# Four of eight experts with 64 token slots, chosen on the chip by token count, and two products for three

## The chip, the core and the metric

The kernel runs on one core of a Trainium2 chip. Its engines work beside each other, each through its own queue in order: TensorE (PE, with its weight loads as PEld) multiplies, VectorE (DVE) and ScalarE (ACT) work elementwise, SyncE (SP) issues the loads, GpSimd (POOL) has next to nothing to do. The metric is the time of one execution in microseconds (us) on the device; lower is better.

## The reference

A trunk of two decoder layers over 256 tokens of width 1024, all in float32. Layer 0 has two mixers and a dense SwiGLU, layer 1 two other mixers and a mixture of experts; each layer ends with a gated embedding, the whole with a norm. The change is in the mixture of experts, which in short is

```python
logits = hn @ w_router                        # 256 x 8
top_val, top_idx = top_k(logits, 2); gates = softmax(top_val)
for each expert e, for the tokens that chose it:
    g, u = split(xt @ w_gate_up[e], 2)        # 1024 -> 2 x 3584
    y = (silu(g) * u) @ w_down[e]             # 3584 -> 1024
    out[token] += gate * y
```

Each of the 256 tokens chooses two of eight experts, so 512 places are spread over them, unevenly. Every expert has 11.0 million weights, 44.04 MB.

## The kernel before

*Precision.* TensorE multiplies float32 at full rate in a rounded form (fp32r). To keep the precision each operand is written as a high part plus a low part: ScalarE casts the high part (`h`, line 145), VectorE subtracts it from the operand (`l`, line 146). A product is then three: high by high, low by high, high by low (`mm3s`, line 182). Every weight passes through these two engines in tiles of 128 x 1024, of which four high and four low ones exist at a time (`SPL_BUFS`). A product marked f32 in the trace (the router, the token counts, the transposes) has plain float32 operands.

*Loads.* SP loads raw weights of 1 MB into 11 buffers (`RAW_BUFS`) in the order in which they are used, through `gate_up_view` and `gate_up_raw` (lines 734 to 758) and `wload` (line 170). A load waits until VectorE has taken the last difference from the buffer's former content. The address of each is fixed when the program is built.

*Routing.* The router's logits `pl` give the two choices of each token, `Mk` (line 1000). Products with a triangular matrix count, for each token, its place among those of its expert: `pos` (line 1010), 0 where it did not choose it. `gather(pair)` (line 1014) makes one-hot matrices `oh` from pos, 128 slots for each of two experts side by side, and multiplies the normed tokens by them (`xg`): the tokens of two experts, transposed, as a high and a low part `xe`. It also transposes the one-hots to `ohT`, by which `combine` (line 1135) puts the results back onto the tokens, weighted by `G` (made in `gates`, line 1053). Surplus tokens beyond 128 in an expert are left to a slow path behind the end of the kernel (`overflow`, line 1220), which runs only if a count exceeds 128.

*The expert loop* (line 1233) takes experts 0 to 7 in order, each in four chunks of 1024, 1024, 1024 and 512 of its 3584 columns. `gate_up` multiplies the tokens (stationary, 128 slots) by the weights into four PSUM banks `mg` and `mu`. `activate` makes silu(g) * u of them (`msg`). `h_T` transposes that in TensorE (`mt`) and splits it into `mhh` and `mhl`. `down` multiplies it by the down weights into two banks `y`. In the program the down products of a chunk follow the gate and up products of the next; `h_T` is called within these, and `activate` in the middle of `down`. The order on each engine is made from this by a planner, when the program is built, from its own estimates of durations; `after(...)` pins some instructions behind others.

The gathers of pairs 1, 2 and 3 are called in experts 1, 3 and 5.

Of the kernel before, what the change touches and what calls it, by code (L numbers as in the profile page):

```python
# [83 lines left out]
def trunk_kernel(  # L84
# [846 lines left out]
    def layer1_moe(pT):  # L931
# [78 lines left out]
        dve.scalar_tensor_tensor(pos, pr, 1.0, Mk, ADD, MUL)  # L1010
        with after("mm"):
            some_products(PRODUCTS[2])

        def gather(pair):
# [11 lines left out]
            xe = parts([P, KT, T], "xT", f"xe{pair}", gp, bufs=XT_BUFS)  # L1026
            for k in range(0, KT, 2):
# [7 lines left out]
                for j in range(2):  # L1035
                    split(sub2(xe, slice(None), k + j), q[:, j, :], scale=pcol("ffn", 8 + k + j))
            q = pt(f"oq{pair}", (P, 2, NB, P))
            for j in range(2):
                for b in range(NB):
                    pe.transpose(q[:, j, b, :], oh[:, b, j, :].bitcast(F32), ident)  # L1040
            ohT = s2(f"ohT{pair}", [P, 2, NB, P], F32R)
            act.copy(ohT, q)
            return xe, ohT

        first = gather(0)
# [5 lines left out]
        cnt, G = sm("cnt", (P, 1), I32), sm("G")  # L1051

        def gates():
# [11 lines left out]
            q = pt("cnt", (P, NE))  # L1065
            for b in range(NB):
                mm(q, ones, Mk[:, b, :], b == 0, b == NB - 1)
            dve.tensor_reduce(cmx, q, AX.X, MAX)
# [15 lines left out]
        def gate_up(e, c, xe, mid):  # L1084
            ns = CHUNKS[c][1] // 512
            banks = [[pa(f"m{nm}{e}{c}{i}") for i in range(ns)] for nm in "gu"]
            xs = slice((e % 2) * P, (e % 2) * P + P)
# [32 lines left out]
        def down(e, c, hT, yb, between):  # L1120
# [3 lines left out]
            for g in range(n // 256):  # L1124
                nm = f"d{e}_{c}_{g}"
                view = WD[e][c0 + g * 256 : c0 + g * 256 + 256].rearrange("(q k) c -> q k c", k=2)
                wt = wload(view, (2, D), nm, spare(nm))
                for i in range(2):
                    mm3s([(yb[half], hT[2 * g + i], sub2(wt[i], slice(None), HALF[half])) for half in range(2)],
                         c == g == i == 0, c == len(CHUNKS) - 1 and g == n // 256 - 1 and i == 1)  # L1130
# [4 lines left out]
        def combine(e, yb, ohT, half):  # L1135
# [9 lines left out]
        yb, xe, hT = {}, {0: first}, {}  # L1145

        def back(e, c, between=None):
            if c == 0:
                yb[e] = [py(f"y{e}{half}") for half in range(2)]
            if (e, c) == (NE - 1, len(CHUNKS) - 1):  # L1150
                part = hT.pop((e, c))
                rows = WD[e][CHUNKS[c][0] :].rearrange("(g q k) c -> g q k c", k=2, q=P)
                for half in range(2):
# [4 lines left out]
                    for k in range(4):  # L1158
                        mm3(yb[e][half], part[k], wt[k], False, k == 3)
# [222 lines left out]
```

## Time and profile before

| | us |
|---|---|
| median of 3 runs | 1547.11 (1545.96 to 1547.27) |
| profiled execution | 1544.88 |
| its span, first to last instruction | 1543.1 |
| TensorE busy | 1514.1 |
| VectorE busy | 1291.4 |
| ScalarE busy | 1070.0 |
| mean granted clock of TensorE | 0.995 |

The busy time of a stretch is a union: two instructions that overlap in the pipe count once, while the mean duration of one instruction contains the overlap. PEclk is the granted clock as a share of 2.4 GHz. "Idle before" is the time that the engine stood just before these instructions, and after the arrow is what ended it. In names the numbers of buffers are left out: `h`, `l` are the parts of the gate and up weights, `h_d`, `l_d` those of the down weights, `r_gu`, `r_d` the raw loads.

### The profile page before, as it was taken

The page shows a single profiled execution, that of the slowest core. Times are in us where ns is not written, and L with a number is a line of the kernel's source. Part 1 is how long each engine was busy: PE and PEld are TensorE (multiplying, and loading weights), DVE is VectorE, ACT ScalarE, POOL GpSimd, SP SyncE. Part 2 cuts the span into 40 slices and gives each one's busy share as a digit, 9 for nine tenths or more (in the row PEclk, how much of TensorE's full clock was granted, in tenths as well). Part 3 has the DMA queues.
Part 4 walks back from the last instruction along what each step waited for, and adds up shares of the span by engine and source line. Part 5 has one row for each costly group of instructions (what it writes and reads, how often), then busy time and mean ns, then how long its engine had stood idle before and what let it go on. Part 6 is the DMA issues. An engine that isn't in the chain of part 4 may idle for free.

```text
span 1543.1 us, 22036 instructions
## 1 busy us (share of the span) xinstructions
PE 1514.1 (98%) x8094; PEld 1299.6 (84%) x8094; DVE 1291.4 (84%) x1703; ACT 1070.0 (69%) x1389; POOL 5.0 (0%) x14
## 2 busy tenths in 40 slices
PE   7999999999999999999999999999999999999996
PEld 7999899988988888888888888888888888888885
DVE  6777655547797899999999899989989989899987
ACT  6545544446556787778878777877777877787765
POOL 0000000000000000000000000000000000000000
PEclk9999999999999999999999999999999999999998
DMA  9514655565534498998999999998998999999951
GB/s 352 221 56 146 208 176 182 190 195 170 181 110 164 164 334 323 407 382 295 359 345 396 347 354 355 353 383 333 377 386 339 341 361 344 397 355 349 389 199 44
DMA packets 136608, 438.27 MB, mean 284 GB/s; under 512 B 9067, under 2 KB 34188, under 8 KB 122412
## 3 DMA queue, kind: packets, MB, share of 16 engines
q1 hardware_dynamic: 132960, 433.19, 75.9%
q10 hardware_dynamic: 3148, 2.31, 0.5%
q0 software_dynamic: 384, 1.29, 0.3%
q8 instruction: 65, 1.06, 0.3%
q14 instruction: 51, 0.42, 0.1%
HBM read 434.92 MB, written 1.84 MB: 283 GB/s over the span
## 4 chain that ended last, share of the span: by engine, by line
PE 85%; DVE 6%; ACT 3%; DMA 3%; issue 2%; ACTq 0%; POOL 0%; DVEq 0%; POOLq 0%
PE mg L174 19%; PE mu L174 18%; PE y L174 17%; PE fu L174 4%; PE fg L174 4%; PE fd L174 4%; PE wo L174 3%; PE pg L174 3%; DMA r_gu<-in_moe_w_gate_up_dram 2%; PE mt L1114 1%; PE p L174 1%; DVE l L146 1%; PE xg L174 1%; DVE l_d L146 1%; PE cb L174 1%
## 5 line engine op out<-in xcount | busy, mean ns | idle before, releaser
L146 DVE TENSOR_TENSOR l<-r_gu,h 128x1024 fp32r<-128x1024 f32 x448 | 529.6, 1220 | 25.4 <-ACT h L145 9.1
L145 ACT CAST h<-r_gu 128x1024 fp32r<-128x1024 f32 x448 | 463.4, 1055 | 87.1 <-PE mu L174 37.5
L146 DVE TENSOR_TENSOR l_d<-r_d,h_d 128x1024 fp32r<-128x1024 f32 x220 | 260.9, 1220 | 12.6 <-ACT h_d L145 3.1
L145 ACT CAST h_d<-r_d 128x1024 fp32r<-128x1024 f32 x220 | 228.5, 1054 | 39.3 <-PE mu L174 19.4
L174 PE MATMUL y<-l_d,mhh 128*128 128x512 f32 x440 | 137.8, 394 | 0.4
L174 PE MATMUL y<-h_d,mhh 128*128 128x512 f32 x440 | 137.3, 393 | 0.0
L174 PE MATMUL y<-h_d,mhl 128*128 128x512 f32 x440 | 135.8, 390 | 0.0
L174 PEld LDWEIGHTS y<-h_d,mhl 128*128 128x128 f32 x440 | 82.6, 188 | 17.7
L174 PEld LDWEIGHTS y<-l_d,mhh 128*128 128x128 f32 x440 | 81.1, 188 | 18.6 <-DVE l_d L146 3.0
L174 PEld LDWEIGHTS y<-h_d,mhh 128*128 128x128 f32 x440 | 81.3, 188 | 17.3 <-ACT h_d L145 1.3
L146 DVE TENSOR_TENSOR l_gu<-r_gu,h_gu 128x1024 fp32r<-128x1024 f32 x44 | 53.8, 1224 | 47.6 <-ACT h_gu L145 47.6
L145 ACT CAST h_gu<-r_gu 128x1024 fp32r<-128x1024 f32 x44 | 46.0, 1048 | 64.2 <-PE fu L174 49.0
L197 ACT CAST mhh<-mt 128x512 fp32r<-128x512 f32 x56 | 32.2, 586 | 63.1 <-PE mt L1114 62.6
L198 DVE TENSOR_TENSOR mhl<-mt,mhh 128x512 fp32r<-128x512 f32 x56 | 37.9, 686 | 29.7 <-ACT mhh L197 29.0
L174 PE MATMUL fg<-x_ffn0h,h_gu 128*128 128x256 f32 x176 | 49.9, 283 | 0.0
L174 PE MATMUL fu<-x_ffn0h,h_gu 128*128 128x256 f32 x176 | 49.9, 283 | 0.0
L174 PE MATMUL fg<-x_ffn0h,l_gu 128*128 128x256 f32 x176 | 49.9, 283 | 0.0
L174 PE MATMUL fu<-x_ffn0l,h_gu 128*128 128x256 f32 x176 | 49.8, 283 | 0.0
L174 PE MATMUL fu<-x_ffn0h,l_gu 128*128 128x256 f32 x176 | 49.8, 283 | 0.0
L174 PE MATMUL fg<-x_ffn0l,h_gu 128*128 128x256 f32 x176 | 49.8, 283 | 0.0
L146 DVE TENSOR_TENSOR l_fd<-r_fd,h_fd 128x1024 fp32r<-128x1024 f32 x22 | 26.9, 1225 | 27.3 <-ACT h_fd L145 26.3
L145 ACT CAST h_fd<-r_fd 128x1024 fp32r<-128x1024 f32 x22 | 23.1, 1052 | 30.5 <-PE fd L174 24.2
(693 smaller groups left out, 3688.2 us busy)
## 6 DMA issues: line engine op xcount, KB each, us to landing
r_gu<-in_moe_w_gate_up_dram SPq DMA_DIRECT2D x192, 1024.0 KB, 7.1
r_d<-in_moe_w_down_dram SPq DMA_DIRECT2D x110, 1024.0 KB, 7.4
r_gu<-in_moe_w_gate_up_dram SPq DMA_DIRECT2D x64, 512.0 KB, 5.6
r_gu<-in_ffn_w_gate_up_dram SPq DMA_DIRECT2D x44, 512.0 KB, 4.5
r_fd<-in_ffn_w_down_dram SPq DMA_DIRECT2D x11, 1024.0 KB, 4.8
r_wo<-in_ev_w_out_dram SPq DMA_DIRECT2D x4, 1024.0 KB, 13.4
r_pg<-in_ple_w_gate_dram SPq DMA_DIRECT2D x4, 1024.0 KB, 4.8
r_wo<-in_od_w_out_dram SPq DMA_DIRECT2D x4, 1024.0 KB, 5.0
```

Source lines behind the costliest of these rows:

```text
L145: last["wcopy"] = act.copy(wh, raw[:, i : i + step])
L146: last["wsplit"] = dve.tensor_tensor(wl, raw[:, i : i + step], wh.bitcast(F32), SUB)
L174: last["mm"] = pe.matmul(o, a, b, start=start, stop=stop, skip_group_check=shared)
L197: last["high"] = act.copy(dst[0], src)
L198: last["split"] = dve.tensor_tensor(dst[1], src, dst[0].bitcast(F32), SUB)
L1114: pe.transpose(q[:, 2 * g + k, :], sg[:, 256 * g + k : 256 * g + 256 : 2], ident)
```

## The change

On the chip experts 1 to 7 are ranked by their token counts; expert 0 keeps its place. The counting products move up from `gates`, and from the ranks a permutation matrix `Pm` is made, by which `pos` and `G` are reordered (`ranked`). `order` writes the ids of the ranked experts into a table; SP loads each into a register (`expert`), and the addresses of all loads of experts 1 to 7 are worked out from it.

The last four in the order, those with the fewest tokens (`few`), get 64 slots each. One gather makes the tokens of all four, with high and low parts side by side: 64 columns high and 64 low in one stationary operand of 128. Two products, by the high and by the low part of the weights, then give all terms, the rows 0 to 63 from the high and 64 to 127 from the low parts of the tokens (`products`). Silu needs their sum: `activate` copies both banks out, and `h_T` multiplies by `both`, two identity matrices of 64 above each other, which transposes and adds; silu, the product with u and the split follow on half the columns. In `combine` the slot matrix has each slot twice (`spread_slots`, called in expert 4), which adds the two halves of y. The limit of the slow path becomes 64 for these four (`cap`).

```diff
+    ids = {}
+
+    def expert(w, e):
+
+        if e == 0:
+            return w[0][0]
+        if e not in regs:
+            regs[e] = nc.values_load(ids["t"][0:1, e - 1 : e], engines=[mybir.EngineType.SP], min_val=1, max_val=NE - 1)
+        return w[0][bass.ds(regs[e], 1)].rearrange("o r c -> (o r) c")
+
+    regs = {}
-        rows = moe_w_gate_up[0][e][k * P : (k + 1024 // n) * P].rearrange("q (j c) -> q j c", j=2)[:, :, c0 : c0 + n]
+        rows = expert(moe_w_gate_up, e)[k * P : (k + 1024 // n) * P].rearrange("q (j c) -> q j c", j=2)[:, :, c0 : c0 + n]
...
+
+        NO = NE - 1
+        pn = pt("cnt", (P, NE))
+        for b in range(NB):
+            mm(pn, ones, Mk[:, b, :], b == 0, b == NB - 1)
         with after("mm"):
             some_products(PRODUCTS[2])
+        key, cmp, rank, Pm = sm("key", (P, NE)), sm("cmp", (P, NO, NO)), sm("rank", (P, NO)), sm("Pm", (P, NO, NO))
+        tmp, posr = sm("tmp", (P, NB, NO, NO)), sm("posr")
+        dve.scalar_tensor_tensor(key, pn, float(NE), iota8, MUL, ADD)
+        dve.tensor_tensor(cmp, key[:, None, 1:].to_broadcast([P, NO, NO]), key[:, 1:, None].to_broadcast([P, NO, NO]), ALU.is_ge)
+        dve.tensor_reduce(rank, cmp, AX.X, ADD)
+        dve.tensor_tensor(Pm, rank[:, None, :].to_broadcast([P, NO, NO]), iota[:, :NO, None].to_broadcast([P, NO, NO]), ALU.is_equal)
+
+        def ranked(dst, src):
+
+            for b in range(NB):
+                dve.tensor_tensor(tmp[:, b], src[:, b, None, 1:].to_broadcast([P, NO, NO]), Pm, MUL)
+            dve.tensor_reduce(dst[:, :, 1:], tmp, AX.X, ADD)
+            dve.tensor_copy(dst[:, :, 0:1], src[:, :, 0:1])
+
+        ranked(posr, pos)
+
+        def order():
+
+            idf, ids["t"] = sm("idf", (P, NO)), sm("ids", (P, NO), I32)
+            dve.tensor_tensor(cmp, Pm, iota8[:, None, 1:].to_broadcast([P, NO, NO]), MUL)
+            dve.tensor_reduce(idf, cmp, AX.X, ADD)
+            dve.tensor_scalar(idf, idf, -1.0, float(NE), MUL, ADD)
+            dve.tensor_copy(ids["t"], idf)
...
-            oh = s2(f"oh{pair}", [P, NB, 2, P], F32R)
+
+            small = few(2 * pair)
+            n_e, n_s = (4, P // 2) if small else (2, P)
+            oh = s2(f"oh{pair}", [P, NB, n_e, n_s], F32R)
             for b in range(NB):
-                for j in range(2):
+                for j in range(n_e):
                     e = 2 * pair + j
-                    last["oh"] = dve.tensor_scalar(oh[:, b, j, :], iota, pos[:, b, e : e + 1], None, ALU.is_equal)
+                    last["oh"] = dve.tensor_scalar(oh[:, b, j, :], iota[:, :n_s], posr[:, b, e : e + 1], None, ALU.is_equal)
-            xe = parts([P, KT, T], "xT", f"xe{pair}", gp, bufs=XT_BUFS)
+            xe = parts([P, KT // 2, n_e, 2, n_s] if small else [P, KT, T], "xT", f"xe{pair}", gp, bufs=XT_BUFS)
...
+                    dst, src = sub2(xe, slice(None), k + j) if not small else None, q[:, j, :]
+                    if small:
+                        x4 = xe[(k + j) // 4][:, (k + j) % 4]
+                        dst, src = (x4[:, :, 0], x4[:, :, 1]), src.rearrange("q (e s) -> q e s", e=n_e)
+                    split(dst, src, scale=pcol("ffn", 8 + k + j))
...
+            def spread_slots():
+                ohT = []
+                for j0 in range(0, n_e, 2):
+                    one = oh.bitcast(F32)[:, :, j0 : j0 + 2]
+                    if small:
+                        twice = s2(f"ot{pair}{j0}", [P, NB, 2, 2, n_s])
+                        for b in range(NB):
+                            act.copy(twice[:, b], one[:, b, :, None, :].to_broadcast([P, 2, 2, n_s]))
+                        one = twice.rearrange("q b e i s -> q b e (i s)")
+                    q = pt(f"oq{pair}{j0}", (P, 2, NB, P))
+                    for j in range(2):
+                        for b in range(NB):
+                            pe.transpose(q[:, j, b, :], one[:, b, j, :], ident)
+                    t = s2(f"ohT{pair}{j0}", [P, 2, NB, P], F32R)
+                    act.copy(t, q)
+                    ohT += [t[:, 0], t[:, 1]]
...
+        gather(0)
+        order()
...
-            q = pt("cnt", (P, NE))
-            for b in range(NB):
-                mm(q, ones, Mk[:, b, :], b == 0, b == NB - 1)
-            dve.tensor_reduce(cmx, q, AX.X, MAX)
+            ranked(Gr, G)
+
+            dve.tensor_scalar(cap[:, 1:], rank, FEW - 0.5, P / 2.0, ALU.is_gt, MUL)
+            dve.memset(cap[:, 0:1], 0.0)
+            dve.tensor_tensor(key, key, iota8, SUB)
+            dve.scalar_tensor_tensor(key, key, 1.0 / NE, cap, MUL, ADD)
+            dve.tensor_reduce(cmx, key, AX.X, MAX)
...
+        def products(e, triples, start, stop):
+
+
+            if not few(e):
+                return mm3s(triples, start, stop)
+            for part in range(2):
+                for o, a, b in triples:
+                    mm(o, a, b[part], start and part == 0, stop and part == 1)
...
-                mm3s([(banks[j][i], sub2(xe, slice(None), k, xs), sub2(wt, slice(None), slice(i * 512, i * 512 + 512))) for i in range(ns)],
-                     k == 0, k == KT - 1)
+                products(e, [(banks[j][i], tokens[e][k], sub2(wt, slice(None), slice(i * 512, i * 512 + 512))) for i in range(ns)],
+                         k == 0, k == KT - 1)
...
+                        if few(e):
+                            res.append([s2(f"ms{nm}{e}{c}{i}", [P, 512]) for nm in "gu"])
+                            for j in range(2):
+                                act.copy(res[i][j], banks[j][i])
+                            continue
...
+                if few(e):
+
+                    q = pt(f"mt{e}{c}{i}", (P, 2, 4, P // 2))
+                    for j in range(2):
+                        for g in range(2):
+                            for k in range(2):
+                                mm(q[:, j, 2 * g + k, :], sg[j][:, 256 * g + k : 256 * g + 256 : 2], both, True, True)
+                    t = s2(f"mgu{e}{c}{i}", [P, 4, P // 2])
+                    act.activation(t, q[:, 0], AF.Silu)
+                    dve.tensor_tensor(t, q[:, 1], t, MUL)
+                    hT = s2(f"mh{e}{c}{i}", [P, 4, 2, P // 2], F32R)
+                    split((hT[:, :, 0], hT[:, :, 1]), t)
+                    res += [hT[:, k].rearrange("q i s -> q (i s)") for k in range(4)]
+                    continue
...
-                mm(q, ohT[:, e % 2, b, :], yp[0], True, False)
-                mm(q, ohT[:, e % 2, b, :], yp[1], False, True)
-                dve.scalar_tensor_tensor(h[:, b, s], q, G[:, b, e : e + 1], h[:, b, s], MUL, ADD)
+                mm(q, slots[e][:, b, :], yp[0], True, False)
+                mm(q, slots[e][:, b, :], yp[1], False, True)
+                dve.scalar_tensor_tensor(h[:, b, s], q, Gr[:, b, e : e + 1], h[:, b, s], MUL, ADD)
...
+        both = sm("both", (P, P // 2))
+        dve.tensor_tensor(both, ident[:, : P // 2], ident[:, P // 2 :], ADD)
...
-                if e % 2 == 1 and c == 2 and e < NE - 1:
-                    xe[e // 2 + 1] = gather(e // 2 + 1)
+                if e % 2 == 1 and c == 2 and e <= FEW - 1:
+                    spread_slots = gather(e // 2 + 1)
+                if (e, c) == (FEW, 1):
+                    spread_slots()
...
+FEW = 4
```

`tokens` and `slots` hold, for each expert, the stationary operands and the transposed one-hots that were `xe` and `ohT`; `combine`, `down` and `back` take them from there.

## Rows read from the trace of the kernel before

**Rows 1.** The page: busy time of each engine, with its share of the span.

```profile
PE 1514.1 (98%) x8094; PEld 1299.6 (84%) x8094; DVE 1291.4 (84%) x1703; ACT 1070.0 (69%) x1389; POOL 5.0 (0%) x14
```

**Rows 2.** Busy time by stretch: us, PE, PEld, DVE, ACT, POOL, PEclk, DMA share, GB/s.

```profile
1255.15:1375.64 120.49, 120.33 (x540) 99.15 (x540) 109.91 (x105) 92.76 (x101) 0.00 (x0) 1.00 0.95 365
...
1009.75:1496.17 486.42, 485.81 (x2197) 400.70 (x2197) 443.86 (x429) 375.03 (x410) 0.00 (x0) 1.00 0.93 356
```

**Rows 3.** The chain that ended last: start, us, what.

```profile
574.48 10.88 PE y L174 x48
```

**Rows 4.** Groups of instructions of one expert (1375.64:1496.17): busy, mean | idle before.

```profile
L146 DVE TENSOR_TENSOR l<-r_gu,h 128x1024 fp32r<-128x1024 f32 x56 | 65.1, 1218 | 1.2 <-ACT h L145 0.3
...
L198 DVE TENSOR_TENSOR mhl<-mt,mhh 128x512 fp32r<-128x512 f32 x7 | 4.8, 689 | 6.1 <-ACT mhh L197 5.9
...
L1114 PE MATMUL mt<-cst,msg 128*128 128x128 f32 x28 | 4.5, 279 | 0.0
...
L197 ACT CAST mhh<-mt 128x512 fp32r<-128x512 f32 x7 | 4.1, 587 | 13.3 <-PE mt L1114 13.3
...
L1143 DVE SCALAR_TENSOR_TENSOR h<-cb,G,h 128x512 f32<-128x512 f32 x4 | 2.8, 745 | 0.9 <-PE cb L174 0.9
```

**Rows 5.** Timelines of ACT and DVE, undisturbed runs.

```profile
1319.18 6.91 ACT L145 CAST h<-r_gu 128x1024 fp32r<-128x1024 f32 x7
...
1343.67 1.07 ACT L1100 ACTIVATE msg<-mg 128x512 f32<-128x512 f32 x2
...
1477.26 6.89 DVE L146 TENSOR_TENSOR l<-r_gu,h 128x1024 fp32r<-128x1024 f32 x6
...
1484.07 4.62 DVE L146 TENSOR_TENSOR l_d<-r_d,h_d 128x1024 fp32r<-128x1024 f32 x4
```

**Rows 6.** What SP's queue waited for: us in total, times, longest.

```profile
SPq L754 <- DVE l L146: 309.0, 135, 5.7
```

**Rows 7.** Busy time by stretch, where several buffers came free.

```profile
620.00:665.00 45.00, 45.00 (x205) 37.45 (x204) 41.33 (x37) 36.23 (x38) 0.00 (x0) 1.00 1.02 413
```

**Rows 8.** The timeline at the router.

```profile
511.65 3.67 PEld L174 LDWEIGHTS pl<-wrt,x_ffn 128*128 128x128 f32 x32 [0.64 <-ACT x_ffn L949]
...
515.53 0.17 DVE L987 TENSOR_REDUCE am<-pl 128x2 f32<-128x16 f32 x1
...
516.18 0.63 PE L174 MATMUL pj<-pwh,pTh 128*128 128x512 f32 x1
...
516.61 0.63 PE L174 MATMUL pj<-pwl,pTh 128*128 128x512 f32 x1
...
517.81 0.18 DVE L1000 TENSOR_TENSOR Mk<-ao,bo 128x16 f32<-128x16 f32 x1
...
520.48 0.17 DVE L1010 SCALAR_TENSOR_TENSOR pos<-prk,Mk 128x16 f32<-128x16 f32 x1 [1.17 <-PE prk L174]
...
520.69 0.88 DVE L1020 TENSOR_SCALAR oh<-cst,pos 128x128 fp32r<-128x128 f32 x4
...
521.54 0.19 PEld L174 LDWEIGHTS xg<-oh,hs00h 128*128 128x128 f32 x1
```

**Rows 9.** Timelines of ACT and DVE, operations on 256 columns.

```profile
524.84 1.94 ACT L200 ACTIVATE xe0h<-xg,prm 128x256 fp32r<-128x256 f32 x5 [0.48 <-PE xg L174]
...
1530.62 0.41 DVE L411 TENSOR_TENSOR pg<-pg,pj 128x256 f32<-128x256 f32 x1
```

**Rows 10.** The timeline of SP: its first load for expert 1.

```profile
599.17 3.27 SPq L754 DMA_DIRECT2D r_gu<-in_moe_w_gate_up_dram  x2
```

**Rows 11.** The line that issues the gate and up loads: ns min/median/max.

```profile
L754 SPq DMA_DIRECT2D r_gu<-in_moe_w_gate_up_dram x192: 539/540/669, 417.1 to 1430.3; - x192
```

**Rows 12.** Busy time by stretch, behind the router's products.

```profile
514.00:515.00 1.00, 1.00 (x11) 1.00 (x10) 0.83 (x6) 0.00 (x0) 0.00 (x0) 1.00 0.00 0
...
516.00:517.00 1.00, 1.00 (x3) 0.75 (x3) 0.83 (x6) 1.00 (x3) 0.00 (x0) 0.50 1.02 156
```

More of the change, by code (lines that the diff above doesn't have):

```diff
@@ L1035, in gather @@
                 for j in range(2):
-                    split(sub2(xe, slice(None), k + j), q[:, j, :], scale=pcol("ffn", 8 + k + j))
-            q = pt(f"oq{pair}", (P, 2, NB, P))
-            for j in range(2):
-                for b in range(NB):
[L1040 to L1045, printed above, removed]
+                    dst, src = sub2(xe, slice(None), k + j) if not small else None, q[:, j, :]
[3 more added lines that the diff above has]
+                    split(dst, src, scale=pcol("ffn", 8 + k + j))
+            for j in range(n_e):
+                s = slice(j * n_s, j * n_s + n_s)
+                if small:
+                    tokens[2 * pair + j] = [xe[k // 4][:, k % 4, j].rearrange("q i s -> q (i s)") for k in range(KT)]
+                else:
+                    tokens[2 * pair + j] = [sub2(xe, slice(None), k, s) for k in range(KT)]
+            def spread_slots():
+                ohT = []
+                for j0 in range(0, n_e, 2):
+                    one = oh.bitcast(F32)[:, :, j0 : j0 + 2]
+                    if small:
+                        twice = s2(f"ot{pair}{j0}", [P, NB, 2, 2, n_s])
[9 more added lines that the diff above has]
+                    ohT += [t[:, 0], t[:, 1]]
+                for j in range(n_e):
+                    slots[2 * pair + j] = ohT[j]
+            if small:
+                return spread_slots
+            spread_slots()
+        slots, tokens = {}, {}
+        gather(0)
+        order()
         with after("mm"):
@@ L1050, in layer1_moe @@
                 copy(*bn)
[L1051 removed]
+        cnt, G, Gr, cap = sm("cnt", (P, 1), I32), sm("G"), sm("Gr"), sm("cap", (P, NE))
         def gates():
@@ L1125, in down @@
                 nm = f"d{e}_{c}_{g}"
-                view = WD[e][c0 + g * 256 : c0 + g * 256 + 256].rearrange("(q k) c -> q k c", k=2)
+                view = expert(moe_w_down, e)[c0 + g * 256 : c0 + g * 256 + 256].rearrange("(q k) c -> q k c", k=2)
                 wt = wload(view, (2, D), nm, spare(nm))
                 for i in range(2):
-                    mm3s([(yb[half], hT[2 * g + i], sub2(wt[i], slice(None), HALF[half])) for half in range(2)],
-                         c == g == i == 0, c == len(CHUNKS) - 1 and g == n // 256 - 1 and i == 1)
+                    products(e, [(yb[half], hT[2 * g + i], sub2(wt[i], slice(None), HALF[half])) for half in range(2)],
+                             c == g == i == 0, c == len(CHUNKS) - 1 and g == n // 256 - 1 and i == 1)
                 if g == n // 512 - 1 and between:
@@ L1133, in down, with combine @@
             return res
-        def combine(e, yb, ohT, half):
+        def combine(e, yb, half):
             s = slice(half * 512, half * 512 + 512)
@@ L1151, in back @@
                 part = hT.pop((e, c))
-                rows = WD[e][CHUNKS[c][0] :].rearrange("(g q k) c -> g q k c", k=2, q=P)
+                rows = expert(moe_w_down, e)[CHUNKS[c][0] :].rearrange("(g q k) c -> g q k c", k=2, q=P)
                 for half in range(2):
@@ L1158, in back @@
                     for k in range(4):
-                        mm3(yb[e][half], part[k], wt[k], False, k == 3)
-                    combine(e, yb[e], xe[e // 2][1], half)
+                        products(e, [(yb[e][half], part[k], wt[k])], False, k == 3)
+                    combine(e, yb[e], half)
                     last_norm[1](half)
@@ L1165, in back @@
                 for half in range(2):
-                    combine(e, yb[e], xe[e // 2][1], half)
+                    combine(e, yb[e], half)
             return res
@@ L1244, in mid @@
                             copy(*bn)
-                activate = gate_up(e, c, xe[e // 2][0], mid)
+                activate = gate_up(e, c, mid)
                 if prev:
```

13 lines of the change are left out of this document (7 added, 6 removed).

## The prediction

> **What bounds the kernel now.** I read the busy line of the page first: TensorE 98%, VectorE 84%, ScalarE 69% of 1543.1 us [rows 1]. Averages over stages decide nothing, so next the table by stretch, cut at one recurring point of the expert loop. One expert is 120.5 us; TensorE is busy for 120.3 of them at granted clock 1.00 (2.4 GHz), VectorE for 109.9, ScalarE for 92.8, and the DMA share is 0.95 at 365 GB/s. The last four steps, experts 4 to 7, are 486.4 us with one gather in them [rows 2]. In the chain of waits a run of 48 matmuls of 512 columns takes 10.88 us, 0.2267 us each [rows 3]. Per expert 504 such products are 114.3 us, 28 transposes at most 4.5 [rows 4] and 8 of the combine 1.8: 120.6, which is the 120.3 but for the overlap. So TensorE bounds this stage, and its pace is the only one fully used.
>
> The next bounds stand close. The groups of one expert [rows 4] give VectorE's work: 56 + 28 differences l of 1024 columns, 7 msg, 7 mhl and the combine. Undisturbed runs give the pace without overlap: six in 6.89 us, four in 4.62, so (6.89 - 1.22)/5 = 1.134 us each [rows 5]; 84 x 1.134 = 95.3, and 16 of 512 columns at 0.60 (0.689 less the same overlap of 0.086) plus 4 h at 0.66 make 107.5. The other 10.6 us VectorE is idle, 6.1 of them before mhl, waiting for ScalarE's mhh, which itself waits 13.3 us for TensorE's mt [rows 4]. The loads: 44.04 MB an expert. SP waits for buffers that VectorE has still to free, 309 us over the run for the gate and up loads alone [rows 6], so loads are late only as far as their consumers are. When several buffers came free together, the DMA moved 413 GB/s for 45 us at share 1.02 [rows 7]: 44.04/0.413 = 106.6 us an expert.
>
> **The change part by part.** *Two products instead of three* in four experts: 168 matmuls fewer, 168 x 0.2267 = 38.1 us of TensorE each. *h_T*: 28 transposes go, 56 true fp32 products of 64 columns come. Such products are two instructions each here: 16 of the router were recorded as 32, at 0.115 us (32 weight loads in 3.67) [rows 8]. 112 x 0.115 = 12.9 us. Bounds: 6.4 if each were one instruction, 25.8 at four; I take 12.9, since the router's row is the same kind of instruction. TensorE then needs 76.2 + 12.9 + 1.8 = 91 us (84 to 104). *VectorE*: msg and mhl, 14 x 0.60, become 14 operations of 256 columns at 0.33 (0.41 less the overlap [rows 9]): 4.6 instead of 8.4, so 104 us. *ScalarE*: casts at (6.91 - 1.05)/6 = 0.976 [rows 5], 82 us; 14 copies of a PSUM bank at 0.48 (two msg in 1.07, less 0.59 for one of 512 columns [rows 4, 5]), 14 operations of 256 columns at 0.37 ((1.94 - 0.47)/4 [rows 9]), 1.0 for yh: 95 us. So a small expert's floor is VectorE's 104 or the loads' 107, not TensorE.
>
> How near will it run to the floor? The lower end is 105: the loads may exceed VectorE's 104 slightly, because landed buffers are in stock. The upper end is 118: VectorE's present idle time of 10.6 stays and the longer h_T (16 fp32 products, 3.7 us for two banks instead of 0.9 for eight transposes at the same pace) puts another 0.9 on each of four waits. Part of the idle time exists only because TensorE is the last: ScalarE runs up to four tiles ahead, then its queue stands at mhh until TensorE has worked these off. That part shrinks. I take 111, VectorE's 104 plus two thirds of today's idle time, which is also 4% above the loads' best. Four experts: 444 instead of 486.4, **-42.4 us**. The third gather (32 products, 4 one-hots, 16 split operations) is inside the 486.4 and goes; its successor in expert 3 has the same 32 products. The doubled slot matrices of expert 4 (four copies of 256 columns, two of 512 on ScalarE, 2.5 us; 8 transposes) lie under VectorE, since ScalarE has 16 us to spare; uncovered they cost 2.5.
>
> *The ranking* stands on the path at the start. Today pos is at 520.48, the one-hots follow at 520.69, and xg starts at 521.54, right behind the last pj product [rows 8]. Between pos and the one-hots come the two counting products, moved up from gates() (four tiny instructions, 0.46) and eight dependent VectorE operations on 7 to 98 elements. The nearest rows: eleven such operations on 2 to 16 elements from 515.53 to 517.81, 0.21 each, and 0.22 for one of 128 columns. 8 x 0.23 = 1.8. The one-hots of the first block are ready 0.3 ahead of xg today, which hides as much: 0.46 + 1.8 - 0.3, **+2.0** (1.5 to 3). *order()*, four operations of 0.2 behind the gather, is 0.8, and eight more in gates() 1.8; VectorE is ahead of TensorE there by part of a tile only, so I take half of these 2.6, **+1.3** (0 to 2.6).
>
> *Addresses in registers.* SP waits once for the table of ids; queued behind it are all loads of experts 1 to 7. The first of these is issued at 599.17 today [rows 10], the table is ready near 531 by my estimate (the gather's end and four operations), so the wait costs nothing: 68 us in hand. Seven register loads and the address arithmetic are not in this trace. Issuing a static load holds SP 0.54 us [rows 11]; with 50 loads an expert SP is a quarter occupied. Cost 0 (0 to 7, a microsecond per register load, hidden as long as the landed stock lasts); it decides only if an issue grew beyond 2 us.
>
> *The end.* Of the 24 products of the last two halves eight go, 1.8 us; the y of the last half wait for VectorE's differences today too, so I take half: **-1** (-2 to 0).
>
> Sum: -42.4 + 2.0 + 1.3 - 1 = -40.1. The profiled execution took 1544.88, 1.8 more than its span: 1504.8. The median of the runs, 1547.11, is 2.2 above it: **1507**.
>
> *Two rules that speak against it.* The loads would be the bound already, if 365 GB/s were all that can be had; the 413 of [rows 7] says no. The Trainium skill, "DMA: Bandwidth & Descriptors", section "Where 436 GB/s comes from", says that for transfers from HBM the HBM side, about 358 GB/s, binds. By that an expert would need an estimated 123 us and nothing could be won (rival 3); the trace does not agree, since its experts already run at 365 and a stretch at 413.
>
> The clock stands at 1.00 in all expert stretches. It fell to 0.50 (1.2 GHz) at 516, right after the router's 32 tiny products had kept the engine formally busy since 511.65 [rows 8, 12]; there a product of 512 columns took 0.43 instead of 0.2267 (516.18 to 516.61 [rows 8]). The h_T of a small expert is a burst of the same kind, and TensorE will idle about a fifth of the time. The skill, "TensorE: Matmul & The Clock Gate", section "A second HAM failure mode: psum-queue depth-cycling", tells of short idle spells between groups of matmuls that make the clock go back and forth; by it rival 4 would hold. No stretch of this trace shows dense products interrupted by such spells.
>
> **The rivals.**
> 1. *Loads or waits hold it up, 115 to 118 an expert.* For: 13.3 us of ScalarE waiting for mt [rows 4], a longer h_T. Against: TensorE is early then. 4 x 116.5 = 466, -20.4 + 2.3: 1529.
> 2. *It meets the floor, 105 to 108.* For: the order of ScalarE's queue was the trouble only with TensorE late. 4 x 106.5 = 426, -60.4 + 2.3: 1489.
> 3. *The loads are the bound today*, 365 GB/s: four experts need 4 x 120.6 = 482, -4.4 + 2.3: 1545, no change. Against: [rows 6, 7].
> 4. *Slower: TensorE falls to 1.2 GHz in the small experts.* 336 x 0.43 + 12.9 + 3.4 = 161 us an expert, 4 x 161 = 644, +158: 1705. It decides from the point where 0.42 of the time is at the low clock: 91 + 0.42 x 70 = 120.5. Below that the experts are no longer than today. For: the burst of tiny products in every h_T. Against: pauses of a few tenths of a microsecond, where the fall of [rows 12] came after a stretch of tiny products alone.
> 5. *The change doesn't do what it says*: were any of the four experts above 64 tokens, the slow path for surplus tokens would run. The reference's routing on the drawn inputs gives 56 for expert 0 and, ranked, 107, 78, 70, 56, 55, 50, 40: none is.
>
> **How the numbers follow.** Forecast (109 to 114 an expert, 1499 to 1519) 0.47; rival 1 0.23; rival 2 0.15; rival 3 0.06; rival 4 0.06, its like on that side that I don't see 0.02; rival 5 0.01. The range takes in rivals 1 and 2 to their ends, 118 an expert (-14.4 + 2.3: 1535) and 105 (-66.4 + 2.3: 1483), and beyond the first three more microseconds for the bounds of the start (1.5 to 5.6) and of the registers: 1483 to 1538, with 0.15 left out. A measurement here can tell about 0.2%, 3 us, from no change. Faster (forecast, rivals 1 and 2) 0.85, same 0.06, slower 0.09.
>
> **What would show it.** Right: in experts 4 to 7 VectorE is busy over 92% of the time and TensorE under 90%, ScalarE's casts wait less for mu and mg, TensorE's weight loads wait for l; the clock stays 1.00; an expert takes 109 to 114 us; experts 1 to 3 keep 120.5; xg starts 2 us later after pos. Wrong: idle time of VectorE above 12 us before the split of h (rival 1), ScalarE waiting for r_gu (loads bound), clock below 0.8 in these experts (rival 4), SP's issues beyond 2 us, or experts 1 to 3 longer than now.

## The result and the profile after

The changed kernel takes 1497.69 us (median of 4 runs, 1497.1 to 1498.93), the kernel before, measured together with it, 1546.53: ratio 0.9689, 95% interval 0.9676 to 0.9702. The forecast was 1507 with a range of 1483 to 1538. The profiled execution took 1497.28, 1.8 more than its span. One execution in the runs below, 1554.7 us in the last experiment, was slower at a lower granted clock, and the ratios leave it out.

The busy line of the page after answers to [rows 1]; the second line is the chain's share by engine, and below it stands the same line of the page before.

```profile
PE 1444.5 (97%) x7726; PEld 1194.7 (80%) x7726; DVE 1268.0 (85%) x1716; ACT 1076.1 (72%) x1441; POOL 4.9 (0%) x14
...
PE 71%; DVE 18%; issue 4%; ACT 4%; DMA 3%; ACTq 0%; DVEq 0%; POOL 0%; POOLq 0%
```

```profile
PE 85%; DVE 6%; ACT 3%; DMA 3%; issue 2%; ACTq 0%; POOL 0%; DVEq 0%; POOLq 0%
```

TensorE still shows 97%, so the busy shares hide the change; the chain doesn't: VectorE's share of it is 18%, where it was 6%, and TensorE's 71% instead of 85%. The table by stretch answers to [rows 2]; its columns are the same. The first two rows are one small expert each, cut at a down product that waits for `l_d` and at the same product one expert later. The third is the stretch ahead of them, with the doubled slot matrices. The last one takes in everything from 1012.07, the point that answers to 1009.75 before, to the first product behind the experts (`pg`).

```profile
1145.35:1254.48 109.13, 104.12 (x456) 73.61 (x456) 104.54 (x105) 95.07 (x115) 0.00 (x0) 1.00 1.02 405
1254.48:1363.61 109.13, 104.17 (x457) 73.64 (x457) 104.55 (x105) 94.93 (x115) 0.00 (x0) 1.00 1.02 404
1012.07:1145.35 133.28, 126.78 (x554) 91.12 (x554) 127.58 (x125) 118.83 (x145) 0.00 (x0) 1.00 1.00 395
...
1012.07:1459.07 447.00, 425.61 (x1877) 303.51 (x1877) 427.50 (x426) 388.99 (x473) 1.07 (x2) 1.00 0.98 388
```

A small expert is 109.13 us instead of 120.49, VectorE is busy for 104.54 of it, ScalarE for 95.07, the granted clock stays 1.00, and the loads come at 405 GB/s with a DMA share of 1.02. The span fell by 47.6 us: +2.3 up to the stretch of the small experts (1009.75 before, 1012.07 after), -49.9 from there to the first product behind the experts (496.9 before, 1009.75 to 1506.69; 447.0 after), and nothing behind it, 36.4 in both.

The groups of one small expert (the first stretch above) answer to [rows 4].

```profile
L146 DVE TENSOR_TENSOR l<-r_gu,h 128x1024 fp32r<-128x1024 f32 x56 | 64.6, 1216 | 0.0
...
L146 DVE TENSOR_TENSOR l_d<-r_d,h_d 128x1024 fp32r<-128x1024 f32 x29 | 33.7, 1217 | 2.4 <-ACT h_d L145 2.4
...
L174 PE MATMUL y<-l_d,mh 128*128 128x512 f32 x56 | 19.6, 431 | 1.1 <-DVE l_d L146 1.1
...
L174 PE MATMUL mt<-both,msg 128*128 128x64 f32 x56 | 8.0, 271 | 0.0
...
L174 PEld LDWEIGHTS mu<-l,xe2l 128*128 128x128 f32 x28 | 4.3, 188 | 6.9 <-DVE l L146 6.9
...
L1212 DVE TENSOR_TENSOR mgu<-mt,mgu 128x256 f32<-128x256 f32 x7 | 3.0, 422 | 2.2 <-ACT mgu L1211 2.2
L198 DVE TENSOR_TENSOR mh<-mgu,mh 128x256 fp32r<-128x256 f32 x7 | 2.9, 418 | 0.0
...
L1211 ACT ACTIVATE mgu<-mt 128x256 f32<-128x256 f32 x7 | 2.7, 383 | 9.5 <-PE mt L174 9.5
```

All of VectorE's idle time stands in two rows, 2.4 before l_d and 2.2 before mgu: 4.6, where it was 10.6. The waits of the same stretch turn the old picture round: the longest are now TensorE's.

```profile
PEld mu L174 <- DVE l L146: 12.3, 21, 0.8
ACT mgu L1211 <- PE mt L174: 9.5, 5, 3.3
PEld y L174 <- DVE l_d L146: 6.8, 15, 1.0
PEld mg L174 <- DVE l L146: 4.2, 11, 0.7
```

The timeline at the router answers to [rows 8]. There 521.54 is the weight load of the first xg; its product began at 521.76:

```profile
521.76 0.28 PE L174 MATMUL xg<-oh,hs00h 128*128 128x256 f32 x1
```

From pos (520.48) to this product it was 1.28 us. After the change it is 2.61, 1.33 more:

```profile
521.86 0.17 DVE L1022 SCALAR_TENSOR_TENSOR pos<-prk,Mk 128x16 f32<-128x16 f32 x1 [1.16 <-PE prk L174]
...
522.31 0.17 DVE L1032 SCALAR_TENSOR_TENSOR key<-cnt,cst 128x8 f32<-128x8 f32 x1 [0.27 <-PE cnt L174]
...
523.74 0.25 DVE L1041 TENSOR_REDUCE posr<-tmp 128x14 f32<-128x98 f32 x1
...
524.03 0.48 DVE L1066 TENSOR_SCALAR oh<-cst,posr 128x128 fp32r<-128x128 f32 x2
...
524.47 0.36 PE L174 MATMUL xg<-oh,hs00h 128*128 128x256 f32 x1 [0.71 <-DVE oh L1066]
```

The register loads and the line of the gate and up loads, answering to [rows 11] (ns, min/median/max):

```profile
L739 SPq TENSOR_LOAD <-ids x7: 265/275/475, 530.7 to 1311.4; - x7
...
L766 SPq DMA_DIRECT2D r_gu<-in_moe_w_gate_up_dram x192: 539/543/663, 418.5 to 1390.3; - x192
...
L766 SPq FUSED_REGOPS  x168: 42/46/56, 599.6 to 1388.6; - x168
L766 SPq MOVE r_gu<-in_moe_w_gate_up_dram x168: 29/29/38, 599.8 to 1388.8; - x168
```

An address from a register costs SP 46 + 29 ns beside an issue of 543, and each of the seven registers 0.28 us for its load and 0.16 for the register operations behind it. Both are lost in SP's waits for buffers.

### The profile page after: what moved, and what is told of

It is laid out like the page before. It is cut to its first block, busy times and chain, and to the rows that moved or that the text cites. A ratio compares the mean times of both kernels' runs of the same rounds, so it can differ in the third digit from the quotient of the medians.

```text
span 1495.5 us, 22012 instructions
## 1 busy us (share of the span) xinstructions
PE 1444.5 (97%) x7726; PEld 1194.7 (80%) x7726; DVE 1268.0 (85%) x1716; ACT 1076.1 (72%) x1441; POOL 4.9 (0%) x14
## 3 DMA queue, kind: packets, MB, share of 16 engines
q8 instruction: 62, 1.02, 0.3%
## 4 chain that ended last, share of the span: by engine, by line
PE 71%; DVE 18%; issue 4%; ACT 4%; DMA 3%; ACTq 0%; DVEq 0%; POOL 0%; POOLq 0%
PE y L174 14%; PE mg L174 11%; PE mu L174 11%; DVE l L146 11%; PE fu L174 4%; PE fg L174 4%; PE fd L174 4%; PE wo L174 3%; PE pg L174 3%; PE mt L174 2%; DMA r_gu<-in_moe_w_gate_up_dram 2%; DVE l_d L146 2%; PE p L174 1%; PE mt L1220 1%; PE in_og L174 1%
## 5 line engine op out<-in xcount | busy, mean ns | idle before, releaser
L145 ACT CAST h<-r_gu 128x1024 fp32r<-128x1024 f32 x448 | 456.6, 1052 | 60.2 <-PE mu L174 22.4
L174 PE MATMUL y<-l_d,mh 128*128 128x512 f32 x216 | 75.3, 430 | 3.7 <-DVE l_d L146 3.7
L174 PE MATMUL y<-l_d,mhh 128*128 128x512 f32 x224 | 69.8, 393 | 0.1
L174 PE MATMUL y<-h_d,mh 128*128 128x512 f32 x216 | 69.2, 402 | 0.3
L174 PE MATMUL y<-h_d,mhh 128*128 128x512 f32 x224 | 69.4, 391 | 0.0
L174 PE MATMUL y<-h_d,mhl 128*128 128x512 f32 x224 | 69.1, 390 | 0.0
L174 PEld LDWEIGHTS y<-l_d,mh 128*128 128x128 f32 x216 | 34.4, 188 | 27.4 <-DVE l_d L146 25.1
L174 PE MATMUL fg<-x_ffn0h,h_gu 128*128 128x256 f32 x176 | 49.9, 283 | 0.0
L174 PE MATMUL fu<-x_ffn0h,h_gu 128*128 128x256 f32 x176 | 49.9, 283 | 0.0
L174 PE MATMUL fg<-x_ffn0h,l_gu 128*128 128x256 f32 x176 | 49.9, 283 | 0.0
L174 PEld LDWEIGHTS y<-h_d,mhl 128*128 128x128 f32 x224 | 42.1, 188 | 8.9
L174 PEld LDWEIGHTS y<-l_d,mhh 128*128 128x128 f32 x224 | 41.5, 188 | 9.5 <-DVE l_d L146 1.4
L174 PEld LDWEIGHTS y<-h_d,mhh 128*128 128x128 f32 x224 | 41.8, 188 | 8.9 <-ACT h_d L145 0.4
```

What stands on the lines that cost most here:

```text
L145: last["wcopy"] = act.copy(wh, raw[:, i : i + step])
L174: last["mm"] = pe.matmul(o, a, b, start=start, stop=stop, skip_group_check=shared)
```

## The experiments

Theory: a small expert lasts as long as VectorE, plus its waits. Rivals: the loads hold it, or TensorE does. Each kernel's ratio is to the kernel before, measured together with it; a difference without a reference is to the 1496.27 that the changed kernel gives in the first of these runs.

**The changed kernel again.** 

> The changed kernel itself, as the mark beside which the three others of this call are read. Both theories: 1498 us, 0.9689 of the kernel before (0.9676 to 0.9702), small experts 109.1 us each.

1496.27, ratio 0.968 (0.9667 to 0.9693).

**Ranking alone.** All experts with 128 slots:

```diff
-FEW = 4
+FEW = 8
-                if e % 2 == 1 and c == 2 and e <= FEW - 1:
+                if e % 2 == 1 and c == 2 and e < NE - 1:
```

> The ranking, the register addresses and the order of the experts stay; all experts keep 128 slots and three products (FEW = 8). Theory (the whole gain is from the third product's going, the ranking only costs): slower than before by the shift seen at the start of the changed kernel, +2 to +4 us, 1549 to 1551; experts 120.5 us each. Rival (part of the gain is from other things, such as the order by count or the addresses): faster than before by over 3 us.

1547.77, ratio 1.0012 (1.0003 to 1.0021): +1.75 against 1546.02, 0.5 to 3.2 by the interval. The ranking is a small cost and no part of the gain; the first xg came 2.61 after pos here too.

**No ranking, the order written into the program.** It leaves out the choice on the chip; the counts are still made, in gates().

```diff
-        if e not in regs:
-            regs[e] = nc.values_load(ids["t"][0:1, e - 1 : e], engines=[mybir.EngineType.SP], min_val=1, max_val=NE - 1)
-        return w[0][bass.ds(regs[e], 1)].rearrange("o r c -> (o r) c")
+        return w[0][ORDER[e]]
...
-        ranked(posr, pos)
+        posr = pos
+ORDER = (0, 5, 2, 4, 7, 3, 1, 6)
```

> The order of the experts by count, which this input has, is written into the program: no permutation, no table of ids, no register loads, fixed addresses; four small experts as in the change. Theory (on-chip choice costs the 2 to 3 us that stand between pos and the gather, the addresses nothing): 2 to 4 us faster than the changed kernel, 1494 to 1496, small experts 109.1 as there. Rival (the register addresses slow the loads): more than 6 us faster, small experts below 108.5.

1496.22, ratio 0.9677 (0.9664 to 0.969): no difference in the median, where 2 to 4 us were expected. Its timeline shows what became of them:

```profile
522.66 0.17 DVE L1020 SCALAR_TENSOR_TENSOR pos<-prk,Mk 128x16 f32<-128x16 f32 x1 [1.16 <-PE prk L174]
...
522.88 0.87 DVE L1057 TENSOR_SCALAR oh<-cst,pos 128x128 fp32r<-128x128 f32 x4
...
523.93 0.28 PE L174 MATMUL xg<-oh,hs00h 128*128 128x256 f32 x1
```

From pos to xg it is 1.27 us again, 1.3 saved; so the choice on the chip costs 1.3 us there. A small expert takes 109.14 here (1144.82 to 1253.96), so the register addresses cost the experts nothing. But pos itself came at 522.66, at 521.86 and 522.32 in two executions of the changed kernel and at 520.48 in the one before [rows 8]. Of the change's instructions only the one that makes `both` stands ahead of it, 0.2 us of VectorE at 504.5 in the changed kernel. All thirteen traces of kernels with the change have pos at 521.40 to 523.55, and of the kernel before there is one trace alone. So why pos comes later, and whether the change moves it, stays open; this part of the 2.3 is unexplained.

**Half the loads.** Half of each weight tile is brought and used twice, in the small experts:

```diff
-            sync.dma_start(raw, view)
+            if half:
+                sync.dma_start(raw[:, 0:1], view[:, 0:1])
...
+            at = slice(0, step) if half else slice(i, i + step)
```

> In the four small experts only the first half of each weight buffer is loaded and read twice: half the bytes, the same work on all engines (the output is wrong by it). Theory (VectorE bounds the small experts): 108 to 109.1 us each as now, total 0 to -4 us, 1494 to 1498. Rival (the loads bound them, DMA share 1.02 at 405 GB/s): they fall to VectorE's 104 to 106, total -12 to -20, 1478 to 1486.

1498.8, ratio 0.9696 (0.9679 to 0.9712). One of its small experts:

```profile
1153.02:1262.17 109.15, 102.72 (x456) 74.17 (x456) 104.34 (x105) 96.53 (x114) 0.00 (x0) 1.00 0.67 203
```

At 203 instead of 405 GB/s the expert still lasts 109.15: it is not the loads that hold it.

**Half of VectorE's differences.** The low part is made for half the columns and used twice:

```diff
-            last["wsplit"] = dve.tensor_tensor(wl, raw[:, i : i + step], wh.bitcast(F32), SUB)
+            if name[0] == "d" and name[1] in "4567" or name[0] in "4567":
+                cut = (slice(None), slice(None), slice(0, 512) if len(shape) == 3 else 0)
+                last["wsplit"] = dve.tensor_tensor(wl[cut], raw[:, i : i + step][cut], wh[cut].bitcast(F32), SUB)
```

> In the four small experts VectorE makes the low part for half of the columns of each tile, and the products use it twice: 84 x 0.53 = 45 us less of VectorE each, loads, casts and products the same (the output is wrong by it). Theory (VectorE bounds, the loads stand 2 us behind it): the small experts fall to the loads' 107 or little over, total -4 to -10, 1488 to 1494. Rival (the loads bound them already): no change, within 2 us of 1498.

1475.03, ratio 0.9541 (0.9525 to 0.9557): -21, twice the gain expected at most (-10). The three complete small experts, one after the other:

```profile
1040.75:1137.89 97.14, 95.30 (x463) 74.51 (x462) 66.25 (x104) 94.14 (x120) 0.00 (x0) 1.00 1.02 410
1137.89:1242.60 104.71, 100.74 (x457) 73.05 (x456) 66.96 (x105) 93.47 (x115) 0.00 (x0) 1.00 1.02 410
1242.60:1351.47 108.87, 103.55 (x457) 72.11 (x456) 66.97 (x105) 94.00 (x116) 0.00 (x0) 1.00 1.02 411
```

In the third of them ScalarE waits for loads:

```profile
ACT h L145 <- DMA r_gu<-in_moe_w_gate_up_dram: 3.2, 5, 1.2
...
ACT h_d L145 <- DMA r_d<-in_moe_w_down_dram: 3.1, 5, 1.4
```

VectorE is busy for 67 us in each (37.6 less than in the changed kernel, where 45 were expected), yet they grow from 97 to 109. The transfers run at 410 GB/s throughout, 39.8 MB in the first stretch (97.14 x 0.410) where an expert takes 44.04: the first experts live on buffers that had landed. When these are used up, the loads' own pace is left, 44.04 MB at 411 GB/s or 107.2 us, 108.87 as measured. ScalarE's waits for loads are 6.3 us there, and 0.9 over all four small experts of the changed kernel. So VectorE, with its waits, holds the small experts at 109.13, and the loads stand right behind it.

**Both halves.** 

> Both together: half the loads and half of VectorE's differences in the four small experts (the output is wrong by it). Both theories: the next bounds, ScalarE's 95 busy and TensorE's 91, with their waits for each other: 97 to 103 us an expert, total -24 to -48, 1450 to 1474. It shows how much would be left behind the two floors.

1438.05, ratio 0.9301 (0.9286 to 0.9317), -58, more than expected.

```profile
1137.13:1231.27 94.14, 92.73 (x457) 76.09 (x457) 66.43 (x105) 91.97 (x115) 0.00 (x0) 1.00 0.75 235
```

94.14, with ScalarE busy for 91.97 and TensorE for 92.73: the third bound, and the forecast's own figures for these two engines (95 and 91).

**The third product back, everywhere.** It repeats the high one, in all products of the small experts:

```diff
-            for part in range(2):
+            for part in range(3):
                 for o, a, b in triples:
-                    mm(o, a, b[part], start and part == 0, stop and part == 1)
+                    mm(o, a, b[part % 2], start and part == 0, stop and part == 2)
```

> A third product, by the high part of the weights once more, is added to all products of the four small experts: TensorE needs 91 + 38 = 129 us each (the output is wrong by it). Theory (what the change won is TensorE's third product, down to the next bound): the small experts are 129 to 131 us, total +80 to +88, 1578 to 1586; ScalarE's wait for mt and VectorE's wait for it grow again to those of the kernel before or more (13 and 6 us an expert). Rival (the products were not the limit, the 64-slot form is): under +40, below 1538.

1581.49, ratio 1.0229 (1.0212 to 1.0246): +85, as the theory said, and so are the waits: ScalarE stands 17.7 us an expert before silu for mt, VectorE 9.4 behind it for mgu.

```profile
1180.26:1310.63 130.37, 129.92 (x625) 109.14 (x624) 107.21 (x105) 96.38 (x115) 0.00 (x0) 1.00 0.90 339
```

TensorE holds the expert again, 129.92 of 130.37. The 64 slots are worth nothing by themselves; the product saved is the whole gain, and this expert is 9.9 us longer than the 120.49 of before, close to the 8.4 by which the forecast had h_T grow (12.9 - 4.5).

**The third product back in down alone**, `products(..., n=3)` in `down` and nowhere else. 

> A third product, by the high part of the weights once more, is added to the down products of the four small experts (56 x 0.2267 = 12.7 us of TensorE each; the output is wrong by it). Theory (VectorE bounds the small experts at 104.5 busy of 109.1, TensorE has some 18 us to spare): 0 to +3 us for each small expert, 1498 to 1510. Rival (TensorE is still beside the bound, as its busy share of 95 per cent says): +10 to +13 for each, 1538 to 1550.

1524.7, ratio 0.9864 (0.9849 to 0.9879): +28.4, 7.1 an expert, between theory and rival. TensorE got 56 x 0.2267 = 12.7 us more, about 104 with the forecast's 91, so no engine is over 105, and the expert still takes 116.34:

```profile
1160.24:1276.58 116.34, 112.63 (x512) 85.68 (x512) 104.99 (x105) 94.63 (x115) 0.00 (x0) 1.00 0.99 378
```

Its waits name the place:

```profile
ACT mgu L1211 <- PE mt L174: 17.2, 7, 4.0
...
DVE mgu L1212 <- ACT mgu L1211: 8.2, 4, 2.9
```

VectorE idles 11.35 us (116.34 - 104.99) instead of 4.6, and 6.0 of these 6.8 are the wait for mgu, 8.2 instead of 2.2. TensorE reaches mt later behind longer down products, ScalarE's silu waits for mt, VectorE stands in its queue behind that. Two engines, each at nine tenths, lose more than either's share where one waits for the other in the middle of its queue.

**A share of the differences to GpSimd.** Every eighth of the small experts:

```diff
-            last["wsplit"] = dve.tensor_tensor(wl, raw[:, i : i + step], wh.bitcast(F32), SUB)
+            at = small_at(name)
+            if at is not None and at % 8 == 4:
+                pool.tensor_tensor(wl, raw[:, i : i + step], wh.bitcast(F32), SUB)
+            else:
+                last["wsplit"] = dve.tensor_tensor(wl, raw[:, i : i + step], wh.bitcast(F32), SUB)
```

> In the four small experts every eighth high-minus-raw difference (11 or so of 85 per expert) is made by GpSimd and not by VectorE; nothing else changes. Theory (a small expert lasts as long as VectorE is busy, 104.5 us, and the loads come next at about 105 to 106): VectorE falls by some 13 us to 91, the expert to 105 to 106, so 3 to 4 us an expert and 12 to 16 us in all, 1480 to 1484. Rival A (VectorE is not the bound, the experts sit at their transfers already): no change, 1495 to 1498. Rival B (GpSimd is several times slower at this than VectorE's 1.2 us, and the stock of four tiles between the engines does not cover one late tile): TensorE waits for the GpSimd tiles and the time rises, above 1500.

1582.05, ratio 1.0242 (1.0217 to 1.0266): +86, rival B. The line's own row (ns, min/median/max), then the timelines of GpSimd and of VectorE at one such difference:

```profile
L156 POOL TENSOR_TENSOR l<-r_gu,h x28: 2368/3248/7602, 1016.6 to 1508.1; 128x1024 fp32r<-128x1024 f32 x28
```

```profile
1179.49 4.61 POOL L156 TENSOR_TENSOR l<-r_gu,h 128x1024 fp32r<-128x1024 f32 x1 [9.30 <-ACT h L153]
```

```profile
1179.51 2.35 DVE L158 TENSOR_TENSOR l<-r_gu,h 128x1024 fp32r<-128x1024 f32 x2
...
1182.14 4.17 DVE L158 TENSOR_TENSOR l<-r_gu,h 128x1024 fp32r<-128x1024 f32 x2
```

GpSimd took 4.61 us, and between 2.37 and 7.6 elsewhere; while it ran, two of VectorE's took 4.17 instead of 2.35. GpSimd's operation began together with VectorE's first two, which kept their 2.35, and went on after them for 2.2 us, about what its shortest takes; VectorE's next two then took 1.8 more. It looks as if the two engines took turns on these operands, but spans on GpSimd are rough, and no run tried GpSimd alone. The table by stretch shows the rest: one expert, then a hole in which TensorE waits for GpSimd's tile, then the products behind it.

```profile
1178.19:1307.94 129.75, 108.31 (x457) 79.45 (x458) 110.82 (x95) 95.25 (x116) 40.26 (x11) 0.93 0.92 341
1082.80:1087.63 4.83, 0.00 (x1) 0.01 (x1) 2.58 (x3) 0.86 (x2) 4.77 (x1) 0.77 0.51 207
1087.63:1092.06 4.43, 4.43 (x11) 3.46 (x11) 1.78 (x2) 3.01 (x3) 0.00 (x0) 0.50 0.69 216
```

VectorE, with ten operations fewer, is busy for 110.82 us instead of 104.54; and after TensorE had stood still for 4.8 us its clock was granted at 0.50 (1.2 GHz) for the next 4.4.

**Expert 0 small as well.** It has 56 tokens and always comes first, so it needs no rank. Its one-hot columns stand twice in the first gather's matrix, which lays its low part beside its high part.

```diff
-            return e >= FEW
+            return e == 0 or e >= FEW
...
+                    if e == 0:
+                        to, cols = to.rearrange("q (i s) -> q i s", i=2), iota[:, None, : P // 2].to_broadcast([P, 2, P // 2])
...
+                        last["high"] = act.activation(dst[0][:, z:], src[:, z:], AF.Copy, scale=sc)
+                        dve.scalar_tensor_tensor(dst[0][:, :z], src[:, z : 2 * z], sc, dst[0][:, z : 2 * z].bitcast(F32), MUL, SUB)
```

> Expert 0 (56 tokens with these inputs, always first, not ranked) gets 64 slots with low and high part side by side and two products too, so five experts of eight run in the new way. Theory (a small expert is bound by the engines' own work, wherever it stands): expert 0 falls from 120.5 to 109 to 111 us, the first gather gets eight more short VectorE instructions (1 to 2 us), so 8 to 11 us less in all, 1485 to 1488. Rival (expert 0 is held by the router's work that runs beside it, the gates, the copies and the order of first products on VectorE): less than 4 us gained, 1492 to 1497.

1482.08, ratio 0.9587 (0.9571 to 0.9603): -14.2, better than both kernels and more than the theory said. From the first xg to the end of expert 0, in this kernel:

```profile
524.03:663.13 139.10, 133.80 (x617) 102.08 (x618) 132.50 (x162) 123.53 (x151) 0.00 (x0) 1.00 0.89 346
```

and in the changed kernel:

```profile
524.47:678.07 153.60, 151.87 (x696) 125.90 (x697) 142.29 (x154) 123.84 (x137) 0.00 (x0) 1.00 0.88 339
```

It is 14.5 us shorter. TensorE, which had 1.7 us free there, hands over to VectorE: TensorE's weight loads for mg and mu now wait 13.5 us for l. VectorE's busy time falls by 9.8 us and its idle time from 11.3 to 6.6. The estimate of 8 to 11 had carried over the 11.4 us between a large and a small expert, less the gather's operations; why VectorE's work falls by 9.8 here, and by 5.4 in the later experts, no run takes apart.

**The second half of h_T one step later.** The products with both stay; silu, the product with u and the split move behind the differences of the next k:

```diff
                 if (k, j) == (MID, 0):
                     mid()
+                if (k, j) == (MID + 1, 0):
+                    mid2()
```

> Only the order of h_T in the small experts: TensorE's products with both stay where they are (ahead of the products of the second k), silu, the product with u and the split of h follow one k later, two tiles of l further down VectorE's and ScalarE's queues. Theory (the 4.6 us in which VectorE idles in each small expert are its and ScalarE's wait for TensorE at h_T, and nothing else separates the expert from VectorE's 104.5): the waits for mgu and h_d fall from 4.6 to under 2, a small expert lasts 106 to 107.5, the loads (44.04 MB at 410 GB/s, 107.4) becoming the limit once the landed stock is used up; 1485 to 1491 in all. Rival A (the loads hold the experts at 109 whatever VectorE does): no change, 1495 to 1498. Rival B (TensorE now waits for h at the start of the down products, because it comes two tiles later): slower than 1499.

1497.33, ratio 0.9684 (0.9668 to 0.9701). This looks like rival A, but it tells nothing: VectorE's timeline has the old order, in the changed kernel

```profile
1169.70 6.89 DVE L146 TENSOR_TENSOR l_d<-r_d,h_d 128x1024 fp32r<-128x1024 f32 x6
1177.18 0.42 DVE L1212 TENSOR_TENSOR mgu<-mt,mgu 128x256 f32<-128x256 f32 x1 [0.59 <-ACT mgu L1211]
1178.12 2.36 DVE L146 TENSOR_TENSOR l_d<-r_d,h_d 128x1024 fp32r<-128x1024 f32 x2 [0.51 <-ACT h_d L145]
```

and in this one

```profile
1171.11 6.89 DVE L146 TENSOR_TENSOR l_d<-r_d,h_d 128x1024 fp32r<-128x1024 f32 x6
1178.58 0.42 DVE L1222 TENSOR_TENSOR mgu<-mt,mgu 128x256 f32<-128x256 f32 x1 [0.58 <-ACT mgu L1221]
1179.52 2.36 DVE L146 TENSOR_TENSOR l_d<-r_d,h_d 128x1024 fp32r<-128x1024 f32 x2 [0.51 <-ACT h_d L145]
```

The planner, which orders the engines' queues from its own estimates, left them where they were. Whether the 4.6 us can be had stays open; by the loads' 107.2 it could be 2 us an expert at most, once the landed buffers are used up.

**Both together.** 

> Both together: expert 0 with 64 slots and two products as well, and the later half of h_T in all five small experts. Theory: the two gains add, 14.2 measured for the first and 5 to 11 for the second: 1471 to 1478. Rival (the loads limit, since five experts now run faster than the DMA can bring their weights, and the stock is used up by the fifth): 1479 to 1483, no better than expert 0 alone.

1481.72 (median of the other three executions), ratio 0.9583 (0.9564 to 0.9603): the gain of expert 0 alone, as it must be when the other edit moved nothing. It doesn't speak for this run's rival.

## Why the prediction was right, and by how much not

*Two products, -42.4.* The mechanism holds: TensorE's third product was the bound, its return brings TensorE back to 129.92 of 130.37, and VectorE is the next one. Forecast and measured: VectorE 104 and 104.54, ScalarE 95 and 95.07. The first is partly luck: the same sum gave 107.5 for the expert before, where [rows 2] have 109.91, so VectorE's work fell by 5.4 us and not by 3.8. The mis-sized term is VectorE's idle time, taken as two thirds of today's 10.6, 7; it was 4.6. That makes 109.13 instead of 111, and over four experts the 7.5 us by which the forecast of this stage (-42.4) fell short of the -49.9. By as much the sum misses the profiled execution, 1504.8 against 1497.28; the other 1.8 of the 9.3 between 1507 and 1497.69 is the distance from profiled execution to median, taken as 2.2 and now 0.4. The reason given, that ScalarE's queue stands at the split of h because TensorE is last, was right, and worth more than half of the 10.6 instead of a third; the run with three down products shows the same wait coming back, 2.2 to 8.2, as TensorE fills up.

*The loads' floor.* Given as 106.6 at 413 GB/s; the stretch that is held by them ran at 411 and took 108.87. So the lower end of 105 would not have been held over four experts, only as long as landed buffers last. VectorE's 104.5 plus 4.6 and the loads' 108.9 came out alike, and nothing in the runs ties them to each other; the runs with half of the one and half of the other tell them apart. With half the loads nothing changes, and with half of VectorE's differences the experts gain only while landed buffers last. Rival 3 took 365 GB/s as all that can be had: four experts at 388, two of them at 404 and 405, refute it. For transfers from HBM the Trainium skill, "DMA: Bandwidth & Descriptors", section "Where 436 GB/s comes from", names about 358 GB/s as what binds; the trace does not agree.

*The ranking, +2.0.* 1.33 between pos and the first product xg, 1.75 as a whole in the kernel that only ranks. *order() and gates(), +1.3*: from pos to the first down products it is 55.25 us (521.86 to 577.11) instead of 53.84 (520.48 to 574.32), 1.41 more, which the ranking's 1.33 all but fills; so these operations are hidden and the term is near 0. That the start came out at +2.3, near the 3.3 of these two terms, is luck: 1.4 of it is pos coming later, for a reason that no run shows. *Addresses, 0*: right, as the run with the order written into the program shows. *The end, -1*: the -49.9 behind 1012 is used up by four experts at 109.1 (-42.4 - 7.5), so nothing is left for it.

*What would show it.* VectorE over 92%: 96%. Weight loads waiting for l: 12.3 + 4.2 us. ScalarE's casts wait 0.4 us an expert for mu and mg, where it was 10.7. The clock: 1.00. Experts 0 to 3 kept their time: 488.0 us from the first xg to the point at 1009.75 before, 487.6 to the one at 1012.07 after. xg 2 us later after pos: 1.3 later. TensorE under 90% was not seen: the table has it at 95% (104.12 of 109.13). But the record of a product lasts 0.39 us and more (431 ns on the mean for y with l_d) where products follow each other every 226.7 ns [rows 3], so the start of each of its pauses counts as busy. What it needs is told by the run with the third product in all products: 129.92 less 168 x 0.2267 is 91.8, the forecast's 91, and 84% of 109.13.

*The rivals.* Loads or waits at 115 to 118: refuted by the 109.13, and half the loads make no difference. The floor of 105 to 108: one microsecond away. The clock: refuted here, 1.00 in every small expert, with waits of at most 1.1 us before a weight load; in the run with GpSimd it was 0.50 after a hole of 4.8 us. The same rule of the Trainium skill that the prediction weighed ("TensorE: Matmul & The Clock Gate", section "A second HAM failure mode: psum-queue depth-cycling") would have had it fall; the trace does not agree for pauses as short as these. The slow path did not run: 36.4 us stand behind the experts, as before.

## What to carry to other kernels

When one engine gives up a third of its work, the gain ends at the next engine's busy time plus that engine's waits, so work out every engine's time and the loads' for one turn of the loop, and expect the waits that exist only because the old bound was last to shrink with it. A first turn that runs faster than the later ones may be living on landed buffers, as here; judge a floor by the last. And after moving an instruction in the program, look at the engine's timeline before reading anything from the time.

## What was not expected of the hardware

GpSimd and VectorE slow each other on these differences: one takes GpSimd 2.37 us at the least, 4.61 in the case shown and up to 7.6, and two of VectorE's took 4.17 us there instead of 2.35. A hole of 4.8 us in TensorE's work was followed by 4.4 us at a granted clock of 0.50. One core drew 410 GB/s through 310 us.
